# Moving the first block's bias lines behind the compression and the first FoX pair

## The chip, the cores and the metric

The kernel runs on one core of one Trainium2 chip. The time is device microseconds (us) of one execution. TensorE (PE, with its weight loads PEld) multiplies matrices, VectorE (DVE), ScalarE (ACT) and GpSimd (POOL) do the elementwise work, and SyncE (SP) issues most of the transfers (DMAs); POOL issues a few. Each engine works through its own instructions in order, and so does the queue from which it issues its DMAs: an instruction that waits for a semaphore holds up all that stand behind it on its engine.

## The reference, cut to what matters

Two transformer-like blocks, the first at sequence 512 and width 1024. The first mixes its tokens in three ways at once and then runs a convolutional feed-forward network; all is float32.

```python
h = rmsnorm(x, norm_g[0]) * (1 + sc_m) + sh_m
p_a, p_b, p_c = split_cols(h @ w_in, ...)
y_a = rwkv7_mix(p_a, ...)          # 4 heads, a recurrent scan over the tokens
y_b = fox_mix(p_b, b_f)            # 6 heads, softmax(q k^T + cum_q - cum_k), causal, 128-row blocks
y_c = nsa_mix(p_c, ..., rel_bias)  # 6 heads: compressed, selected and window attention
x = x + g_m * rmsnorm(concat(y_a, y_b, y_c) @ w_out, ...)
```

In `nsa_mix`, keys and values are first compressed (`gelu(flat @ w1) @ w2`, 31 compressed positions), and all logits get a bias that depends on the distance of two tokens alone: `rel_bias[t5_bucket(dist)]`, one value per head and distance. `mod`, from which `sc_m`, `g_m` and the like are cut, is `silu(c) @ ada_w`.

## The kernel before, in words

A float32 matrix product is made as three products of high and low parts (`uh`, `ul`, `whi`, `wlo`). A scheduler places the instructions: it takes the order in which the program names them as their priority, so that the program's order settles which of several ready instructions goes first on an engine, and the order of an engine's queue is fixed when the kernel is built.

The change lies in the RWKV stage of the first block, some 145 to 376 us into the span. The loop `while cores` (L1130) runs there in turns. A turn advances the two RWKV scans (`core(0)`, `core(1)`; their small matmuls go to PSUM tiles `psr`), adds matmuls of a projection as filler (`fill`, tiles `psm`, 128x512 outputs), every second turn one column group of `mod` (`some_ada`: 512 KB of weights into `raw`, products on DVE and on POOL, L507 and L508, adding up in `am`, and a matmul into `psr`), and takes NS = 3 steps of the list `side`. A step is what lies between two `yield`s of a generator. `side` holds, one behind the other:

- `compress`: for the keys and then the values, load `kcv` from SBUF into `kk2` (L970, L971), add position vectors on POOL (`kr`, L975), load four weight tiles `w1` (L980), and multiply (`psa<-kr,w1`).
- `fox(0)`, `fox(1)`, `fox(2)`: two heads each. For each of four blocks of 128 query rows and each head: logits into a PSUM tile of bank s (`pss<-fk,fq`, with 128, 256, 384 and 512 keys), minimum and bias on DVE (L1028), exponential on ACT, reciprocal on DVE, scaling on POOL (L1093), PE transposes into bank s (`pss<-cm,p`, L1052), a copy out (`pt`), and after both heads the product with the values (`psa<-pt,fv`). Bank s has two buffers.
- `stacks`: stacked copies of keys for NSA.

Ahead of the loop `decays(spare)` (L938) makes FoX's cumulated decays, `cum`, which go to DRAM (`dcum`, L958) and come back as bias tiles `fb` (L1081). Its last three statements are what the change moves:

- `lines("1", ...)` (L457): a table `lines1` of 33 rows, with one column per distance, comes in four chunks (512, 512, 512 and 96 columns: `lo<-in_lines`, L467), is cast on DVE (L469), multiplied on PE with the high and the low part of `rel_bias` (`pss<-lo,rb1h` and `rb1l`, 6 rows out, in bank s), copied by ACT (`lo<-pss`), and written to DRAM as `d1` (`d<-lo`, L475).
- `load_cb()` (L930): eight small DMAs on SP from `d1` to the tile `cb` (L935).
- `skew("k1", ...)` (L479): one DMA on POOL's queue that copies `d1` 128 times (1917 KB) into the DRAM tensor `k1`.

`cb` and `k1` are read in `nsa(j)`, behind the loop (L1174 and the `soften` of the compressed logits), from some 380 us on. The tiles named `lo`, `kk2`, `kr`, `w1`, `pt` come from `spare`, which hands out the RWKV stage's own tiles, five buffers in turn. `OR` is 0, so that `compress` stands first in `side`. The function `bias_1` is new with the change.

Of the kernel before, what the change touches and what calls it, by code (L numbers as in the profile page):

```python
# [279 lines left out]
def two_blocks(ctx, tc, ins, out):  # L280
    nc = tc.nc
    S, V, G, PE = nc.scalar, nc.vector, nc.gpsimd, nc.tensor
    def mm(o, l, r, start=True, stop=True):
        PE.matmul(o, l, r, start=start, stop=stop)  # L284

    def act(o, i, f, **kw):
        S.activation(o, i, f, **kw)  # L287

    def tt(o, a, b, op):
        V.tensor_tensor(o, a, b, op=op)  # L290

    def ts(o, a, s1, s2, op0, op1=ALU.bypass):
        if s2 is None:
            V.tensor_scalar(o, a, s1, None, op0=op0)
        else:
            V.tensor_scalar(o, a, s1, s2, op0=op0, op1=op1)

    def stt(o, a, s, b, op0, op1):
        V.scalar_tensor_tensor(o, a, s, b, op0=op0, op1=op1)  # L299
# [24 lines left out]
    def vc(name, i=0, n=1):  # L324
        s = VECS[name].start
        return vec[:, s + i:s + i + n]
# [129 lines left out]
    def lines(name, pool, o_tile, pst, rb, n, h, dst):  # L456

        l = pool.tile([33, h], F32, name="rb" + name)
        V.memset(l[32:33, :], 1.0)
        nc.sync.dma_start(l[:32, :], ins[rb])  # L460
        hi, lo = [pool.tile([33, h], F32R, name="rb" + name + c) for c in "hl"]
        act(hi, l, AF.Copy)
        tt(lo, l, hi.bitcast(F32), SUB)
        for j in range(0, n, 512):
            m = min(512, n - j)
            o = o_tile(F32)[:33, :m]
            nc.sync.dma_start(o, ins["lines" + name][:, j:j + m])  # L467
            E = o_tile(F32R)[:33, :m]
            (V if name == "1" else G).tensor_copy(E, o)  # L469
            ps = pst()[:h, :m]  # L470
            mm(ps, hi, E, True, False)
            mm(ps, lo, E, False, True)
            o = o_tile(F32)[:h, :m]
            act(o, ps, AF.Copy)
            nc.sync.dma_start(dst[:, j:j + m], o)  # L475

    def skew(name, src, row0, rows, rstep, off, n):

        d = dram.tile([rows, P, n], F32, name=name)  # L479
        s = src[:]  # L480
        w = s.shape[1]
        G.dma_start(d, bass.AP(tensor=s.tensor, offset=s.offset + row0 * w + off, ap=[[rstep * w, rows], [0, P], [1, n]]))
        return d
# [94 lines left out]
    def bank(tag, n):  # L578
        return psm.tile([P, T], F32, name="ps" + tag, tag="p" + tag, bufs=n)
# [328 lines left out]
    def project(jobs):  # L908
        for j in jobs:
            yield from j  # L910
# [22 lines left out]
    def load_cb():  # L933
        for p1 in range(8):
            nc.sync.dma_start(cb[p1 * 16:(p1 + 1) * 16],  # L935
                              bass.AP(tensor=d1[:].tensor, offset=d1[:].offset + LN + 7 - p1,
                                      ap=[[LC, 16], [E1_N, 6], [1, 55]]))

    def decays(spare):

        cf = spare("cf")[:, :P]
        nc.sync.dma_start(cf, ins["cmat"][:, CM["causT"]])
        V.tensor_copy(cmask[:, :P], cf)
        V.tensor_copy(cmask[:, P:], ident)
        ps = bank("s", 2)
        for b in range(NB):
            PE.transpose(ps[:6, b * P:(b + 1) * P], ffl[:, b], ident)
        f = spare("ff")
        act(f[:6], ps[:6], AF.Identity, bias=vc("b_f")[:6])
        na = spare("fa")  # L950
        act(na[:6], f[:6], AF.Abs)
        act(na[:6], na[:6], AF.Exp, scale=-1.0)
        act(na[:6], na[:6], AF.Ln, bias=1.0)
        stt(f[:6], f[:6], 0.0, na[:6], MIN, SUB)
        V.memset(na[:6], 1.0)
        cum = spare("cum")
        V.tensor_tensor_scan(cum[:6], na[:6], f[:6], 0.0, op0=MUL, op1=ADD)
        nc.sync.dma_start(dcum, cum[:6])  # L958
        lines("1", keep, lambda dt: spare("lo", dt), lambda: bank("s", 2), "rel_bias", E1_N, 6, d1)
        load_cb()  # L960
        k1.append(skew("k1", d1, 0, 6, 1, 0, LN))

    def compress(spare):

        for j, nm in enumerate(("k", "v")):
            pe = vc("pe_" + nm, 0, 16)
            krs = [spare("kr") for _ in range(2)]
            for g in range(2):
                kk = spare("kk2")
                nc.sync.dma_start(kk[0:64], kcv[j][H2[g]])  # L970
                nc.sync.dma_start(kk[64:128, :T - 1], kcv[j][H2[g], 1:])  # L971
                kv = kk.rearrange("p (c j l) -> p c j l", j=8, l=2)[:, :, :, 0].rearrange("p c j -> p j c")
                for a in range(2):
                    kr = krs[a][:, :496].rearrange("p (j g c) -> p j g c", g=2, c=31)
                    G.tensor_tensor(kr[:, :, g], kv[:, :, a:a + 31],  # L975
                                    pe[:, 8 * a:8 * a + 8, None].to_broadcast([P, 8, 31]), op=ADD)
            ps = bank("a", 1)
            for q in range(4):
                w1 = spare("w1")
                nc.sync.dma_start(w1, ins[f"c{nm}1"][:, q * T:(q + 1) * T])  # L980
                for a in range(4):
                    yield
                    mm(ps[:, :62], w1[:, a * P:(a + 1) * P], krs[q // 2][:, (4 * (q % 2) + a) * 62:(4 * (q % 2) + a + 1) * 62],
                       q + a == 0, q + a == 6)
            yield
            w2 = st.tile([P, 64], F32, name="w2")
            nc.sync.dma_start(w2, ins[f"nsa_c{nm}_w2"])
            h = st.tile([P, 62], F32, name="ch")
            V.tensor_copy(h, ps[:, :62])
            u = st.tile([P, 62], F32, name="cu")  # L990
            tt(u, h, h, MUL)
            ts(u, u, 0.044715, 1.0, MUL, ADD)
            tt(u, u, h, MUL)
            act(u, u, AF.Tanh, scale=math.sqrt(2.0 / math.pi))
            ts(u, u, 0.5, 0.5, MUL, ADD)
            tt(h, u, h, MUL)
            ps = bank("a", 1)
            if j == 0:
                for g in range(2):
                    mm(ps[H2[g], :31], w2, h[:, g * 31:g * 31 + 31])  # L1000
                V.tensor_copy(kct, ps[:, :31])
            else:
                for g in range(2):
                    mm(ps[:31, g * 64:g * 64 + 64], h[:, g * 31:g * 31 + 31], w2)
                V.tensor_copy(vcn.rearrange("c g d -> c (g d)"), ps[:31, :128])
        ts(gates[:, 0, 0:18:3], gates[:, 0, 0:18:3], valid, None, MUL)
# [55 lines left out]
    def stack_k(src, tiles, *room):  # L1062

        hl = parts(src, *room)
        r = []
        for s in range(2):
            k = tiles[2 * s:2 * s + 2]
            for a, b in zip(k, hl):
                nc.sync.dma_start(a[0:64].bitcast(F32), b[H2[s]].bitcast(F32))
                nc.sync.dma_start(a[64:128].bitcast(F32), b[H2[s]].bitcast(F32))  # L1070
            r.append(k)
        return r
# [30 lines left out]
    def stacks(spare):  # L1103
        for _ in work[0]:
            pass
        ka = [keep.tile([P, T], F32R, name="ksw", tag=t) for t in ("kcv0", "kcv1", "fk0", "fk1", "fk2")]
        kb = keep.tile([P, 3, T], F32R, name="ksw3", tag="fv")
        for src, tiles in ((ks, ka[:4]), (kw, [ka[4], *(kb[:, i] for i in range(3))])):
            kst.append(stack_k(src, tiles, *(spare("s" + c, F32R) for c in "hl")))
            yield  # L1110

    kst = []
    prep, core, spare = rwkv(phA.enter_context(tc.tile_pool(name="rp", bufs=1, reuse_waits="tile")))
# [7 lines left out]
    nm[0] = 1  # L1121
    work[0] = project(jobs[NA:])
    decays(spare)
    side = [*(fox(j, spare) for j in range(3))]
    side.insert(OR, compress(spare))
    side.append(stacks(spare))
    side = project(side)
    turn = [0]
# [876 lines left out]
```

## Time and profile before

| | |
|---|---|
| median of 3 runs | 2211.7 us (2207.88 to 2213.74) |
| profiled execution | 2211.9 us, span 2210.1 us |
| PE busy | 2137.1 us, 97% of the span |
| DVE, ACT, POOL busy | 1167.0, 799.1, 465.2 us |
| mean granted TensorE clock | 0.977 |

PE busy counts a matmul that runs at the lower of the clock's two levels (1.2 and 2.4 GHz, shown as 0.5 and 1.0) as busy for its longer time. In the rows below, the same matmul therefore appears with two durations, and a stretch's column PEclk is the mean of the level granted in it. Names are shown without their buffer numbers: `w` is `w1`, `cb<-d` reads `d1`, `k<-d` is `k1<-d1`, `raw<-in_ada_dram` a group of `mod`'s weights. `psa<-kr,w` counts each matmul in two parts.

### The profile page before, as it was taken

Reading aid. Unit: us, or ns where it says so; the run is one execution under the profiler, and the core shown is the slowest. Engines: PE = TensorE matmul, PEld = TensorE weight load, DVE = VectorE, ACT = ScalarE, POOL = GpSimd, SP = SyncE. Lnnn points to the kernel's source line nnn. Section 1 sums busy time; section 2 is a strip of 40 time slices with the busy share of each in tenths; the row PEclk is TensorE's granted clock in tenths of the full one; section 3 lists DMA queues with packets and bytes.
Section 4 is the critical chain, followed back from the end, with each engine's and each line's share of the span. In section 5 each row is a group of like instructions: output and inputs, shape, how many; then the busy total and the mean of one; then the engine's idle time right before and its main releaser. Section 6 shows DMA issues by size and latency. Waiting matters only on the chain.

```text
span 2210.1 us, 31599 instructions
## 1 busy us (share of the span) xinstructions
PE 2137.1 (97%) x12444; PEld 1764.5 (80%) x12444; DVE 1167.0 (53%) x2217; ACT 799.1 (36%) x1358; POOL 465.2 (21%) x459
## 2 busy tenths in 40 slices
PE   5988999997999999899999999999999999999999
PEld 4867776766788888888888889998877888888887
DVE  8563544567653464654344439967655455433442
ACT  5432323452543343432222325445453233222221
POOL 5044342325000000321011023343221022100110
PEclk9988998997999999999999999999999999999999
DMA  7245334200452222132222343243162223222222
GB/s 271 91 139 184 106 125 123 88 1 32 151 182 96 95 96 98 55 113 97 95 95 96 120 142 112 93 138 95 67 186 70 101 84 101 102 96 96 95 96 86
DMA packets 84975, 238.32 MB, mean 108 GB/s; under 512 B 14032, under 2 KB 21510, under 8 KB 84698
## 3 DMA queue, kind: packets, MB, share of 16 engines
q1 hardware_dynamic: 79098, 226.41, 30.5%
q0 software_dynamic: 5008, 9.31, 1.2%
q8 instruction: 98, 1.61, 0.3%
q10 hardware_dynamic: 720, 0.57, 0.1%
q14 instruction: 51, 0.42, 0.1%
HBM read 216.02 MB, written 15.33 MB: 105 GB/s over the span
## 4 chain that ended last, share of the span: by engine, by line
PE 91%; DVE 4%; DMA 3%; ACT 1%; issue 1%; POOL 1%; SPq 0%; DVEq 0%; ACTq 0%; POOLq 0%
PE mm L284 67%; PE psm L284 6%; PE psr L284 4%; PE pS L284 3%; PE pss L284 2%; PE pso L284 2%; PE pO L284 2%; PE k L284 1%; PE psa L284 1%; PE pT L1590 1%; PE pst L1052 1%; DMA aw<-in_ada_dram 1%; DMA raw<-in_wst_dram 1%; PE pT L1573 1%; DVE ul L299 1%
## 5 line engine op out<-in xcount | busy, mean ns | idle before, releaser
L273 ACT ACTIVATE whi<-raw 128x1024 fp32r<-128x1024 f32 (+4 forms) x314 | 327.6, 1046 | 815.7 <-PE mm L284 622.9
L274 DVE TENSOR_TENSOR wlo<-raw,whi 128x1024 fp32r<-128x1024 f32 (+4 forms) x302 | 370.7, 1229 | 337.8 <-ACT whi L273 325.0
L284 PE MATMUL mm<-ul,whi 128*128 128x512 f32 (+1 forms) x1296 | 501.9, 388 | 5.5 <-DVE ul L299 5.5
L284 PE MATMUL mm<-uh,wlo 128*128 128x512 f32 (+1 forms) x1296 | 501.5, 388 | 1.0 <-DVE wlo L274 1.0
L284 PE MATMUL mm<-uh,whi 128*128 128x512 f32 (+1 forms) x1296 | 496.6, 388 | 4.3 <-ACT uh L287 3.3
L284 PEld LDWEIGHTS mm<-ul,whi 128*128 128x128 f32 x1296 | 244.9, 189 | 58.5 <-DVE ul L299 8.2
L284 PEld LDWEIGHTS mm<-uh,whi 128*128 128x128 f32 x1296 | 243.3, 189 | 56.0 <-ACT uh L287 4.7
L284 PEld LDWEIGHTS mm<-uh,wlo 128*128 128x128 f32 x1296 | 244.9, 189 | 50.9 <-DVE wlo L274 1.9
L284 PE MATMUL mm<-hh,wlo 128*128 128x512 f32 (+1 forms) x550 | 209.3, 381 | 0.0
L284 PE MATMUL mm<-hl,whi 128*128 128x512 f32 (+1 forms) x550 | 209.3, 381 | 0.0
L284 PE MATMUL mm<-hh,whi 128*128 128x512 f32 (+1 forms) x550 | 208.4, 381 | 0.0
L1441 POOL TENSOR_TENSOR gg<-gg,R 128x512 f32<-128x512 f32 x44 | 77.5, 1763 | 473.4 <-ACT gg L287 473.4
L284 PE MATMUL mm<-whi,uh 128*128 128x256 f32 (+1 forms) x488 | 140.5, 288 | 0.0
L284 PE MATMUL mm<-whi,ul 128*128 128x256 f32 (+1 forms) x488 | 139.8, 287 | 0.0
L284 PE MATMUL mm<-wlo,uh 128*128 128x256 f32 (+1 forms) x488 | 139.2, 285 | 0.0
L284 PEld LDWEIGHTS mm<-hl,whi 128*128 128x128 f32 x550 | 103.4, 188 | 19.8
L284 PEld LDWEIGHTS mm<-hh,wlo 128*128 128x128 f32 x550 | 103.4, 188 | 19.7
L284 PEld LDWEIGHTS mm<-hh,whi 128*128 128x128 f32 x550 | 103.4, 188 | 19.7
L287 ACT ACTIVATE p<-p,smin 128x128 f32<-128x128 f32 (+4 forms) x136 | 81.8, 602 | 82.3 <-DVE smin L1028 45.8
L290 DVE TENSOR_TENSOR gh<-mm,gg 128x512 f32<-128x512 f32 x44 | 30.4, 691 | 130.5 <-PE mm L284 124.9
L284 PEld LDWEIGHTS mm<-whi,ul 128*128 128x128 f32 x488 | 93.1, 191 | 1.7 <-issue 1.5
L284 PEld LDWEIGHTS mm<-whi,uh 128*128 128x128 f32 x488 | 93.0, 191 | 1.4 <-issue 0.4
(509 smaller groups left out, 3419.3 us busy)
## 6 DMA issues: line engine op xcount, KB each, us to landing
raw<-in_wst_dram SPq DMA_DIRECT2D x294, 512.0 KB
raw<-in_ada_dram SPq DMA_DIRECT2D x32, 512.0 KB
aw<-in_ada_dram SPq DMA_DIRECT2D x16, 512.0 KB
raw<-in_wst_dram SPq DMA_DIRECT2D x8, 448.0 KB
ka<-d POOLq DMA_DIRECT2D x1, 3570.0 KB, 51.5
k<-d POOLq DMA_DIRECT2D x1, 2556.0 KB, 20.6
part<-in_x_dram SPq DMA_DIRECT2D x4, 512.0 KB
xa<-in_x_dram SPq DMA_DIRECT2D x8, 256.0 KB
```

The lines of the kernel that those rows point to most:

```text
L273: nc.scalar.activation(hi[:, :n], w, AF.Copy)
L274: (e or nc.vector).tensor_tensor(lo[:, :n], w, hi[:, :n].bitcast(F32), op=ALU.subtract)
L284: PE.matmul(o, l, r, start=start, stop=stop)
L287: S.activation(o, i, f, **kw)
L290: V.tensor_tensor(o, a, b, op=op)
L299: V.scalar_tensor_tensor(o, a, s, b, op0=op0, op1=op1)
L1052: PE.transpose(ps[:, j:j + P], p[:, j:j + P], ident)
L1441: G.tensor_tensor(g, g, R, op=MUL)
L1573: PE.transpose(ps[:, (j * nb + b) * P:(j * nb + b + 1) * P], xn[:, (b * n + j) * P:(b * n + j + 1) * P], ident)
L1590: PE.transpose(ps[:, j:j + P], p[:, o + j:o + j + P], ident)
```

## The change

Three statements of `decays` become a generator `bias_1`, which goes into `side` at position 2: behind `compress` (0) and `fox(0)` (1), ahead of `fox(1)`. It has two steps: the lines, and then `load_cb` with `skew`.

```diff
         V.tensor_tensor_scan(cum[:6], na[:6], f[:6], 0.0, op0=MUL, op1=ADD)
         nc.sync.dma_start(dcum, cum[:6])
+
+    def bias_1(spare):
+
         lines("1", keep, lambda dt: spare("lo", dt), lambda: bank("s", 2), "rel_bias", E1_N, 6, d1)
+        yield
         load_cb()
         k1.append(skew("k1", d1, 0, 6, 1, 0, LN))
+        yield
 
     def compress(spare):
...
     side = [*(fox(j, spare) for j in range(3))]
     side.insert(OR, compress(spare))
+    side.insert(2, bias_1(spare))
     side.append(stacks(spare))
```

The number of instructions stays the same; their order changes. Line numbers behind `decays` grow by five (L975 is what L970 was), and buffer numbers by a constant in each part. The first place is SP's queue at the head of the stage, with the last writes of `d1`, the eight `cb` loads and the compression's loads. Before:

```order
L475 DMA d1_93<-lo_1216 6x512
L497 DMA raw_2048<-in_ada_dram 128x1024
L497 DMA raw_2054<-in_ada_dram 128x1024
L970 DMA kk2_1276<-kcv0_109 64x512
L475 DMA d1_93<-lo_1226 6x96
L971 DMA kk2_1276<-kcv0_109 64x511
L497 DMA raw_2280<-in_ada_dram 128x1024
L935 DMA cb_654<-d1_93 16x6x55 x8
L970 DMA kk2_1281<-kcv0_109 64x512
L971 DMA kk2_1281<-kcv0_109 64x511
L980 DMA w1_1287<-in_ck1_dram 128x512
L980 DMA w1_1342<-in_ck1_dram 128x512
```

And now, nearer to the queue's start:

```order
L975 DMA kk2_1219<-kcv0_109 64x512
L976 DMA kk2_1219<-kcv0_109 64x511
L497 DMA raw_1675<-in_ada_dram 128x1024
L958 DMA dcum_653<-cum_1179 6x512
L975 DMA kk2_1224<-kcv0_109 64x512
L976 DMA kk2_1224<-kcv0_109 64x511
L985 DMA w1_1230<-in_ck1_dram 128x512
L985 DMA w1_1285<-in_ck1_dram 128x512
```

The first weight tiles of the compression have gone 18 rows up in the queue, ahead of everything that `lines` and `load_cb` issue, and stand behind `dcum` and the loads of `kk2`.

The second place is PE, where the first matmuls of the compression stand among those of the RWKV scans. Before:

```order
L284 MATMUL psr1_1776<-X_1498,part_89 64x64 x11
L284 MATMUL psa_1286<-kr_1274,w1_1287 128x62 x4
L284 MATMUL psa_1286<-kr_1274,w1_1342 128x62 x4
L284 MATMUL psr1_1776<-X_1498,part_89 64x64 x3
```

And now:

```order
L284 MATMUL psr0_1322<-part_89,pr0_113 64x128 x8
L284 MATMUL psr1_1332<-part_89,pr1_114 64x128 x4
L284 MATMUL psa_1229<-kr_1217,w1_1230 128x62 x4
L284 MATMUL psa_1229<-kr_1217,w1_1285 128x62 x4
L284 MATMUL psr1_1332<-part_89,pr1_114 64x128 x4
```

The `psa` rows have gone 62 rows up PE's order, to the scans' 64x128 matmuls.

The third place is POOL's queue between `fox(0)` and `fox(1)`; `p_2602` and `p_2617` are `fox(1)`'s first two scalings. Now:

```order
L507 TENSOR_SCALAR raw_3286<-raw_3286,sil_79 128x256 x3
L508 TENSOR_TENSOR am1_3042<-am1_3042,raw_3049 128x256 x3
L512 TENSOR_TENSOR am1_3042<-am0_3041,am1_3042 128x256
L482 DMA k1_2548<-d1_93 768x1x639
L508 TENSOR_TENSOR am1_3279<-am1_3279,raw_3286 128x256 x3
L512 TENSOR_TENSOR am1_3279<-am0_3278,am1_3279 128x256
L507 TENSOR_SCALAR raw_3489<-raw_3489,sil_79 128x256 x3
L1098 TENSOR_SCALAR p_2602<-p_2602,srec_2607 128x128
L508 TENSOR_TENSOR am1_3482<-am1_3482,raw_3489 128x256 x2
L1098 TENSOR_SCALAR p_2617<-p_2617,srec_2622 128x128
```

Before, the `k1` DMA stood 41 rows further up, at the head of the stage, among the additions for `am1_1731`. On PE the four pairs of `pss<-lo` now stand between `fox(0)`'s last `psa<-pt,fv` and `fox(1)`'s first logits, which stood ahead of that `psa` before. Behind the last filler matmul of the loop, PE now has `fox(1)`'s last logits, its last two groups of transposes and all eight logits and transposes of `fox(2)`; before it had `fox(2)`'s last four logits and five groups of transposes.

## Rows read from the trace of the kernel before

**Rows 1.** The page, parts 1 and 4: busy time, chain of waits.

```profile
PE 2137.1 (97%) x12444; PEld 1764.5 (80%) x12444; DVE 1167.0 (53%) x2217; ACT 799.1 (36%) x1358; POOL 465.2 (21%) x459
...
PE 91%; DVE 4%; DMA 3%; ACT 1%; issue 1%; POOL 1%; SPq 0%; DVEq 0%; ACTq 0%; POOLq 0%
```

**Rows 2.** Windows: length, then busy of five engines, PEclk, DMA share, GB/s.

```profile
180.00:220.00 40.00, 32.87 (x381) 28.99 (x381) 11.13 (x28) 8.22 (x13) 17.34 (x28) 0.74 0.61 186
...
300.00:340.00 40.00, 38.12 (x397) 28.57 (x392) 19.66 (x56) 10.23 (x22) 16.21 (x26) 0.96 0.45 155
340.00:380.00 40.00, 38.37 (x274) 24.61 (x274) 17.87 (x44) 13.57 (x27) 11.23 (x11) 0.79 0.32 91
```

**Rows 3.** Waits of PE, 140 to 400 us: total, times, longest.

```profile
PE psa L284 <- DMA w<-in_ck_dram: 7.1, 1, 7.1
...
PE pss L1052 <- POOL p L1093: 1.9, 2, 1.7
```

**Rows 4.** The chain that ended last, 160 to 200 us: start, duration, piece.

```profile
173.92 7.72 DMA d<-lo
...
181.69 5.33 DMA cb<-d
...
188.23 3.28 DMA w<-in_ck_dram
```

**Rows 5.** Timeline of PE, 150 to 216 us: start, duration, instruction, idle before.

```profile
157.86 1.96 PE L284 MATMUL psr<-part,pr 64*64 64x128 f32 x32
```

**Rows 6.** Timeline of PE behind the wait for `w`.

```profile
191.65 3.64 PE L284 MATMUL psa<-kr,w 128*128 128x62 f32 x16 [7.13 <-DMA w<-in_ck_dram]
...
196.43 0.63 PE L284 MATMUL psm<-ul,whi 128*128 128x512 f32 x1
...
209.62 0.39 PE L284 MATMUL psm<-ul,whi 128*128 128x512 f32 x1
```

**Rows 7.** Timeline of SP's queue, 145 to 200 us.

```profile
151.29 0.29 SPq L958 DMA_DIRECT2D dcum<-cum  x1
```

**Rows 8.** Timeline of POOL, 145 to 200 us.

```profile
183.00 1.42 POOL L975 TENSOR_TENSOR kr<-kk,vec 128x248 f32<-128x248 f32 x2 [1.26 <-DMA kk<-kcv]
```

**Rows 9.** Groups by line and form, 145 to 200 us: busy, mean ns, idle before.

```profile
L284 PE MATMUL pss<-lo,rb1l 33*6 33x512 f32 x3 | 1.4, 470 | 0.0
```

**Rows 10.** DMA issues, 140 to 200 us: count, KB each, us to landing.

```profile
k<-d POOLq DMA_DIRECT2D x1, 1917.0 KB, 21.6
```

**Rows 11.** Timeline of DVE, 170 to 190 us.

```profile
176.51 0.35 DVE L294 TENSOR_SCALAR am<-raw,sil 128x256 f32<-128x256 f32 x1 [4.26 <-DMA raw<-in_ada_dram]
...
185.98 0.74 DVE L294 TENSOR_SCALAR am<-raw,sil 128x256 f32<-128x256 f32 x1 [7.56 <-POOL am L512]
```

**Rows 12.** Timeline of PE at 308.7 us and behind it.

```profile
308.71 0.55 PE L1052 MATMUL pss<-cm,p 128*128 128x128 f32 x3 [1.69 <-POOL p L1093]
```

**Rows 13.** Timeline of PE and POOL, two FoX steps with 384 and 512 keys.

```profile
249.76 0.91 PE L284 MATMUL pss<-fk,fq 64*128 64x384 f32 x2
252.52 0.59 POOL L1093 TENSOR_SCALAR p<-p,srec 128x384 f32<-128x384 f32 x1 [0.18 <-DVE srec L1036]
254.22 1.12 PE L284 MATMUL pss<-fk,fq 64*128 64x512 f32 x2
257.51 0.70 POOL L1093 TENSOR_SCALAR p<-p,srec 128x512 f32<-128x512 f32 x1 [4.40 <-PE psr L284]
```

**Rows 14.** Timeline of PE, the stage's end: last filler, last FoX step, next stage.

```profile
344.78 0.39 PE L284 MATMUL psm<-uh,wlo 128*128 128x512 f32 x1
...
365.37 2.07 PE L284 MATMUL pss<-fk,fq 64*128 64x512 f32 x2
...
371.95 1.09 PE L1052 MATMUL pss<-cm,p 128*128 128x128 f32 x4
373.84 1.97 PE L284 MATMUL psa<-pt,fv 128*64 128x128 f32 x14 [0.80 <-DVE pt L1046]
...
376.31 0.79 PE L284 MATMUL psm<-uh,whi 128*128 128x512 f32 x1
```

## The prediction

> **What bounds the kernel now.** I read the page first: PE is busy for 97% of the span and holds 91% of the chain of waits [rows 1], so a change of order can move the time only where PE stands idle or runs at the lower level of its clock. The table by stretches shows where that is in the RWKV stage. From 180 to 220 us PE is idle for 7.1 of 40 us, and the granted clock has a mean of 0.74; from 300 to 340 us 1.9 us are idle at a mean of 0.96; from 340 to 380 us 1.6 us at 0.79 [rows 2]. The list of PE's waits names the causes: one wait of 7.1 us of the compression's matmuls for the DMA of `w`, and two for POOL's scaling of `p`, 1.9 us together [rows 3]. The chain of waits follows the long one back: the last write of `d1` takes 7.72 us to land, SP stands on the `cb` loads that wait for it until 181.69, these and the `kk` loads behind them go out up to 188.23, and `w` then takes 3.28 us [rows 4]. The reader should see that PE waits for a transfer that is short but was issued late, behind one that nobody needs for another 190 us.
>
> PE then goes on at the lower level: a filler matmul takes 0.63 us at 196.43 and 0.39 at 209.62 [rows 6]. A mean of 0.74 over 40 us, with levels 1.0 and 0.5, is 20.8 us at the lower one; 7.1 of these were the wait itself, so 13.7 us of work ran at half speed and lost 6.9 us.
>
> **The change, part by part.** The sum is made against the profiled execution: 2211.9 us, of which 2210.1 are span; the median of 2211.7 is 0.2 below it.
>
> *What it removes.* Neither `d1`'s writes nor the `cb` loads stand ahead of the compression's loads now. `dcum`, which stands just ahead of them, was issued at 151.29 [rows 7]; two `kr` additions take 1.42 us [rows 8], and `w` lands 3.28 us after its issue [rows 4]. With the loads of `kk` issued some us earlier and landed by then, I estimate `w` at 151.3 + 0.3 + 1.4 + 3.3, about 156.5 us. PE comes to the moved `psa` in the middle of the row that began at 157.86 [rows 5], which itself comes earlier by the first pair of `lines` matmuls, about 1 us. So the wait ends between 0 and 1 us long. Term: -7.1 for the wait and -6.9 for the clock, -14.0 together. Its bounds are 0, if a wait of the same kind comes back further on, and -14.0.
>
> *What comes back at once.* The compression's second half (the values) needs the same tiles of `spare` again; its loads of `kk` wait for `kr` tiles, which are free only when PE has used up the first half. Their trip (`kk`, `kr`, `w`) has no slack in the new order, where PE wants the result after about 20 us. Bounds: 0, and the 7.1 us that the same kind of wait cost before [rows 3]. I take +3, somewhat nearer to 0, since no long transfer of `d1` stands in that trip.
>
> *The lines themselves.* The eight matmuls of some 0.47 us [rows 9], the casts and the copies are the same ones in another place. On PE they cost the same; a chunk's trip is hidden by the filler between two pairs of `pss<-lo`. 0, with 0.5 either way, the wait for `lo` that exists now being of that size.
>
> *POOL and the DMA queues between* `fox(0)` *and* `fox(1)`. The `k1` DMA now stands in POOL's queue in front of `fox(1)`'s first scaling, and waits there for writes of `d1` to land, one of which took 7.72 us [rows 4]. Behind it on POOL are three additions for `am1_3279`, the scaling of `raw_3489` (which waits for its own load) and then `p_2602`, for which PE's first transposes of `fox(1)` wait; behind these the next loads of `raw` on SP, since they want the tiles back. No row of before shows POOL held up right ahead of a FoX step for long. The nearest is the wait of 1.69 us at 308.71 [rows 12]; with it goes a mean clock of 0.96 over 40 us, 1.6 us more [rows 2], so 3.3 in all. The farthest is DVE's wait of 7.56 us for POOL while `k1` was under way [rows 11]. Two first scalings are at risk: bounds 0 and 2 x (7.6 + 1.6) = 18.4. I take two times the nearest row, +6.6.
>
> A second reason lies in the transfers. `k1` took 21.6 us to land [rows 10], and while it was under way DVE waited 4.26 us for a load of `raw` [rows 11]; until now this ran beside a stage with slack on DVE, and now it runs beside FoX. The Trainium skill, page "DMA: Bandwidth & Descriptors", section "Issuing engines are not separate DMA queues", says that DMAs of all issuing engines run on the same 16 DMA engines and interleave, so that POOL's queue gives `k1` no road of its own. By that rule the slow `raw` loads move with `k1` to the new place, and the term stands; if `k1` had a road of its own, the later of the two waits and its 3.3 us would go. The wait of 4.26 us agrees with the rule, without proving it.
>
> *The end of the stage.* `side` is a chain: two more steps behind `fox(0)` put `fox(1)` and `fox(2)` later against the filler matmuls, which are used up earlier. Behind the last filler there now stand nine FoX steps instead of the five of before, and nothing but the scans' own work beside them. A step with 384 keys takes 3.35 us from its logits at 249.76 to the end of its scaling [rows 13], and three transposes take 0.55 [rows 12]: 3.9 us. One with 512 keys takes 3.99 from 254.22 [rows 13], and four transposes by the same measure some 0.7: 4.65. By that slope of 0.75 I estimate 3.15 and 2.4 us for 256 and 128 keys. Nine steps are 4.65 + 2 x (2.4 + 3.15 + 3.9 + 4.65) = 32.9, and the last `psa` 1.97: 34.8 us, against 31.5 us from 344.78 to 376.31 before [rows 14], so +3.3. But the PE work of four more steps, which I estimate at 6 us (logits of 0.5 to 1.1, transposes and `psa` of about as much), leaves the stretch ahead of the last filler: -2.7. The other bound: at the lower clock the last step took from 365.37 to 373.04, 7.7 us instead of 4.65 [rows 14], 1.65 times as much; if the four last steps (17.1 us) ran so without cover, 11.1 us more, or +8.4. I take +3.
>
> *Sum.* -14.0 + 3 + 6.6 + 3 = -1.4: 2210.5, rounded to **2210 us** on the scale of the median.
>
> **The rivals.** A measurement of this kernel can tell about 0.3% from no change, 6.6 us.
>
> *Given back only at the tail (faster).* POOL's queue is held up no longer than PE has other work: the scans' matmuls between `fox(1)`'s first logits and its transposes cover it, as they cover all FoX steps but two now [rows 3]. Then -14.0 + 0 to 3 for the values' half, 0 at POOL, and -2.7 to +3 at the tail. The middle is about -12: 2200 us, from 2195 to 2205. For it: DVE and POOL are far from full. Against it: POOL works in order, and `k1` waits for `d1` now in front of a scaling.
>
> *POOL held up behind* `k1` *(slower).* If the write of `d1` for which `k1` waits lands as late as before (7.72 us) and each of `fox(1)`'s two first scalings comes late by the farthest row, the zone costs +18.4 and with the rest 2222 us; with the tail's upper bound, 2228. This decides as soon as the two waits are together more than about 15 us. For it: the long wait of DVE for POOL in just such a constellation. Against it: that row is DVE's wait, not PE's, and no row shows two such waits one after the other.
>
> *The change doesn't do what it says.* The late `w` stays, since the values' half waits instead: 7.1 us and the clock come back, the removal is worth 0, and the zone and the tail stand alone: 2211.9 + 6.6 + 3, 2221 us. For it: the same five tiles are handed round in `spare`. Against it: no `d1` write stands in front of those loads any more.
>
> **How the numbers follow.** My forecast, the return of most of the gain, has a chance of 0.46, with a range of its own from 2203 to 2218; the faster rival 0.31, `k1` 0.14, the wait that stays 0.09. Of the forecast's chance 0.03 lie on the faster side and 0.03 on the slower. The faster rival's 0.31 count as 0.29 faster and 0.02 the same; the two slower ones' 0.23 as 0.20 slower and 0.03 the same. Faster 0.32, within 0.3% 0.45, slower 0.23. The range takes in the forecast and the nearer part of the rivals, 2199 to 2222.
>
> **What would show it.** In the profile of the changed kernel the wait of `psa<-kr,w` for `w` should be gone, and the filler matmuls behind it should take 0.39 us from the start; that is the part I am surest of. SP should issue `w` by about 154 us. POOL should show a gap ahead of `k1` and the list of PE's waits a longer `pss<-cm,p` for `p` at `fox(1)`'s start, 3 to 4 us twice with the clock. From the last filler to the next stage's first should be 33 to 40 us. The forecast is wrong if `fox(1)`'s first transposes wait for less than 1 us (then faster), or if `psa` waits for `w` again in the values' half by more than 5 us (then slower).

## The result: slower by 1.0%, and the profile after

| | before | changed |
|---|---|---|
| median, us | 2209.82 (4 runs, same chip) | 2234.98 (4 runs) |
| ratio, 95% interval | | 1.0101 [1.0086, 1.0115] |
| span of the profiled execution, us | 2210.1 | 2233.7 |
| mean granted TensorE clock | 0.977 | 0.969 |

The prediction was 2210 us within 2199 to 2222. The measured time lies outside, on the slower side. The ratios, here and below, are those on record for the fast executions and not quotients of the medians (1.0114 here); one execution of e4_kct_act (2661.89 us) and one of e13_last_chunk_end (11735.5 us) are left out of them.

All of the difference arises in the RWKV stage. Here is the table by stretches of both kernels, cut where each begins the next stage's matmuls (columns as in [rows 2]); first the kernel before:

```profile
145.00:376.30 231.30, 216.08 (x2541) 163.47 (x2539) 110.54 (x280) 69.54 (x141) 96.11 (x140) 0.90 0.42 138
...
620.00:2210.10 1590.10, 1577.53 (x8116) 1333.97 (x8114) 801.87 (x1359) 554.72 (x837) 256.14 (x191) 1.00 0.31 103
```

The changed kernel, the stage as a whole, and then what follows some 244 us behind its end, as above:

```profile
145.00:401.20 256.20, 225.08 (x2536) 169.40 (x2536) 110.28 (x280) 69.33 (x140) 95.21 (x139) 0.83 0.38 123
...
645.00:2233.70 1588.70, 1575.28 (x8113) 1332.48 (x8111) 800.30 (x1359) 554.43 (x836) 255.37 (x191) 1.00 0.31 103
```

The stage is 24.9 us longer, with the same instructions. PE is idle for 31.1 us in it, where it was 15.2: 15.9 us. It is busy for 225.1 us, where it was 216.1, since the mean clock fell from 0.90 to 0.83: 9.0 us. From there to the end of the span it is 1832.5 us, where it was 1833.8.

The same view of the changed kernel, cut at the places where something happens:

```profile
145.00:187.80 42.80, 31.02 (x444) 26.29 (x444) 27.49 (x53) 10.96 (x17) 28.94 (x36) 0.86 0.63 197
...
271.40:312.00 40.60, 29.54 (x347) 22.50 (x347) 10.94 (x30) 10.24 (x23) 15.50 (x24) 0.80 0.45 149
...
349.80:401.20 51.40, 45.31 (x325) 27.04 (x323) 19.87 (x59) 16.10 (x36) 13.06 (x17) 0.67 0.21 62
```

The last of these stretches, in the kernel before:

```profile
344.78:376.30 31.52, 29.89 (x242) 18.09 (x240) 15.06 (x38) 10.54 (x21) 9.10 (x9) 0.77 0.27 78
```

Three stretches stand out: the compression's end (187.8), the stretch between `fox(0)` and `fox(1)`, with 11.1 us of idle PE, and the end of the stage, 51.5 us from the last filler to the next stage instead of 31.5 [rows 14], at a mean clock of 0.67 instead of 0.77. PE's waits by what ended them, 140 to 430 us, answer to [rows 3]:

```profile
PE pss L1057 <- POOL p L1098: 10.1, 5, 2.8
PE psa L284 <- DVE kct L1006: 7.4, 1, 7.4
PE psr L284 <- DVE MT L290: 6.3, 1, 6.3
...
PE psa L284 <- DVE pt L1051: 2.8, 2, 2.0
PE psa L284 <- DMA w<-in_ck_dram: 1.2, 1, 1.2
```

The wait for the keys' `w`, 7.1 us in [rows 3], is down to 1.2. In its place stands one of 7.4 us for `kct`, and those for `p`, `MT` and `pt` did not exist in this size.

**The compression.** From the timelines of SP, POOL, DVE and PE of the changed kernel, in that order:

```profile
169.97 6.72 SPq L497 DMA_DIRECT2D raw<-in_ada_dram  x3
176.86 0.47 SPq L975 DMA_DIRECT2D kk<-kcv  x1
...
181.69 1.39 POOL L980 TENSOR_TENSOR kr<-kk,vec 128x248 f32<-128x248 f32 x2 [3.66 <-DMA kk<-kcv]
183.04 2.32 POOL L508 TENSOR_TENSOR am<-am,raw 128x256 f32<-128x256 f32 x3
...
186.20 0.35 DVE L294 TENSOR_SCALAR am<-raw,sil 128x256 f32<-128x256 f32 x1 [7.77 <-POOL am L512]
187.50 0.18 DVE L1006 COPY kct<-psa 128x31 f32<-128x31 f32 x1
...
187.79 1.51 PE L284 MATMUL psa<-kr,w 128*128 128x62 f32 x6 [7.44 <-DVE kct L1006]
```

Read it from the bottom. PE waits for the copy of `kct`, which frees the one buffer of bank a. The copy takes 0.18 us, but stands on DVE behind a product for `am`, which waits for POOL, which waits for the values' `kk`, which SP issued at 176.86 behind three loads of `raw`. It is a wait of the same length as the one removed, 4 us earlier in the span. The granted clock falls during the wait in both kernels. In the windows of the kernel before (first the wait's beginning, then the work behind it):

```profile
184.50:187.70 3.20, 0.02 (x1) 0.00 (x0) 1.65 (x4) 0.00 (x0) 2.00 (x3) 1.00 0.32 81
...
191.70:208.20 16.50, 16.50 (x140) 14.76 (x142) 5.07 (x11) 2.82 (x3) 6.05 (x11) 0.50 0.70 224
```

And in the changed kernel, behind its wait:

```profile
187.80:200.00 12.20, 12.20 (x95) 10.40 (x97) 2.54 (x6) 3.13 (x5) 4.44 (x7) 0.50 0.58 189
```

It is at the lower level once more from 224.0 to 230.7 us, with 6.2 us of work. Half of such work is lost time: some 8 us before, some 9 now.

**Between fox(0) and fox(1).** From the timelines of POOL, DVE and PE:

```profile
282.75 1.33 POOL L482 DMA_DIRECT2D k<-d  x1 [6.56 <-DMA d<-lo]
299.11 1.39 POOL L507 TENSOR_SCALAR raw<-raw,sil 128x256 f32<-128x256 f32 x3 [11.37 <-DMA raw<-in_ada_dram]
...
295.09 0.35 DVE L294 TENSOR_SCALAR am<-raw,sil 128x256 f32<-128x256 f32 x1 [9.72 <-DMA raw<-in_ada_dram]
...
287.77 0.45 PE L284 MATMUL pss<-fk,fq 64*128 64x128 f32 x2
297.66 0.47 PE L284 MATMUL psr<-WU,pr 64*64 64x64 f32 x2 [6.28 <-DVE MT L290]
300.90 0.47 PE L1057 MATMUL pss<-cm,p 128*128 128x128 f32 x1 [2.76 <-POOL p L1098]
```

DVE stands for 9.72 us on a load of `raw`, with `MT` of the scans behind it, for which PE waits. POOL stands for 11.37 us on the next load, with `fox(1)`'s `p` behind it. And `fox(1)`'s first logits come at 287.77 us, 68.6 us behind `fox(0)`'s first:

```profile
219.15 0.48 PE L284 MATMUL pss<-fk,fq 64*128 64x128 f32 x2
```

Before, the two were 43.2 us apart:

```profile
224.94 0.49 PE L284 MATMUL pss<-fk,fq 64*128 64x128 f32 x2
...
268.18 0.49 PE L284 MATMUL pss<-fk,fq 64*128 64x128 f32 x2
```

From 272 to 291 us, where the four links run, PE has no wait at all: it works off the scans and filler.

**The end.** PE's timeline, last filler, last FoX steps, next stage:

```profile
349.75 0.40 PE L284 MATMUL psm<-uh,wlo 128*128 128x512 f32 x1
...
384.80 0.90 PE L1057 MATMUL pss<-cm,p 128*128 128x128 f32 x3 [1.79 <-POOL p L1098]
...
396.87 1.11 PE L1057 MATMUL pss<-cm,p 128*128 128x128 f32 x4 [2.19 <-POOL p L1098]
...
401.23 0.80 PE L284 MATMUL psm<-uh,whi 128*128 128x512 f32 x1
```

Nine FoX steps run behind the last filler; their logits stand at 350.68, 356.56, 359.64, 362.74, 366.51, 373.13, 380.52, 385.63 and 391.77 us. Three of the last four steps wait for their own chain (logits, minimum, exponential, scaling), and PE is idle for 6.1 us of the stretch, where it was 1.6. From 367.4 us to its end, 33.8 us, the granted clock is at its lower level, where it was so for 14.4 us before (from 361.9): four transposes take 1.11 us, like the 1.09 in [rows 14].

### The profile page after: what moved, and what is told of

It reads as the page before. It is cut to its first block, busy times and chain, and to the rows that moved or that the text cites. A ratio compares the mean times of both kernels' runs of the same rounds, so it can differ in the third digit from the quotient of the medians.

```text
span 2233.7 us, 31606 instructions
## 1 busy us (share of the span) xinstructions
PE 2144.7 (96%) x12444; PEld 1768.9 (79%) x12444; DVE 1165.5 (52%) x2217; ACT 800.6 (36%) x1358; POOL 464.6 (21%) x459
## 4 chain that ended last, share of the span: by engine, by line
PE 89%; DVE 5%; DMA 3%; POOL 1%; ACT 1%; issue 1%; SPq 0%; DVEq 0%; POOLq 0%; ACTq 0%
PE mm L284 66%; PE psm L284 5%; PE psr L284 3%; PE pS L284 3%; PE pss L284 2%; PE pso L284 2%; PE pO L284 2%; DMA raw<-in_ada_dram 1%; PE k L284 1%; PE pT L1596 1%; PE pst L1057 1%; PE psa L284 1%; DMA aw<-in_ada_dram 1%; DVE am L299 1%; DVE ul L299 1%
```

## The experiments

All stand against the kernel before on the same chip, whose median in these sessions was 2212.3 to 2212.8 us, some 3 us above the one in the result; a time that misses an expected range by less than that says little. In the table, *gap* is the time from `fox(0)`'s first logits to `fox(1)`'s, *end* that from the last filler to the next stage, *compression* the sum of PE's waits ahead of `psa<-kr,w`, all from the profiled execution, in us.

| kernel | links between fox(0) and fox(1) | k1 issued at | gap | end | compression | ratio [95%] |
|---|---|---|---|---|---|---|
| before | 0 | 165.2 | 43.2 | 31.5 | 7.1 | 1 |
| changed | 4 | 282.8 | 68.6 | 51.5 | 8.6 | 1.0101 [1.0086, 1.0115] |
| e4_kct_act | 4 | as changed | 68.0 | 51.5 | 8.1 | 1.0100 [1.0082, 1.0117] |
| e6_double | 4 | 163.8 | 67.1 | 50.0 | 8.6 | 1.0073 [1.0050, 1.0096] |
| e19_bank_a | 4, in bank a | 282.2 | 45.2 | 42.8 | 7.2 | 1.0023 [1.0013, 1.0034] |
| e7_one_link | 1 | 274.8 | 53.1 | 38.9 | 3.1 | 1.0012 [1.0003, 1.0021] |
| e16_in_fox1 | 0 (1 in fox(1)) | 309.2 | 47.7 | 35.3 | 4.3 | 1.0023 [1.0012, 1.0034] |
| e17_in_fox2_early | 0 (1 in fox(2)) | 338.3 | 47.3 | 37.0 | 2.6 | 0.9993 [0.9984, 1.0002] |
| e15_in_fox2 | 0 (1 in fox(2)) | 345.5 | 46.3 | 34.4 | 3.9 | 0.9982 [0.9972, 0.9993] |
| e13_last_chunk_end | 0 | 163.4 | 43.8 | 31.8 | 6.6 | 0.9984 [0.9973, 0.9995] |
| e10_mid | 0 | 207.5 | 63.7 | 33.0 | 8.9 | 1.0041 [1.0027, 1.0055] |
| e5_last | 0 | 381.2 | 46.7 | 40.1 | 9.5 | 1.0088 [1.0072, 1.0105] |

A link is one chunk of `lines`: load, cast, two matmuls, copy, write.

**e4_kct_act: is it the copy's place in DVE's queue?** The changed kernel with

```diff
-                V.tensor_copy(kct, ps[:, :31])
+                act(kct, ps[:, :31], AF.Copy)
```

> The changed kernel with one edit: the compressed keys (kct) are copied out of PSUM by ACT instead of DVE. In the changed kernel the values' half of the compression waits 7.4 us for that copy, which stands on DVE behind an addition for am that waits for POOL. Theory A (the copy's place in DVE's queue makes the wait): the wait falls below 2 us, and with the clock the time falls by 7 to 13 us, to 2222 to 2228. Rival (the operands kr and w of the values' half come late anyway): the wait stays at 5 us or more under another name, and the time stays within 3 us of 2235.

2235.83 us, ratio 1.0100, the same as the changed kernel. The rival holds. The wait of PE has another name and the same length:

```profile
186.60 1.51 PE L284 MATMUL psa<-kr,w 128*128 128x62 f32 x6 [7.11 <-DMA w<-in_cv_dram]
```

The profile puts a wait down to what came last. Here two things came almost together, and taking one away moved nothing: the values' `kk`, `kr` and `w` follow one another, and the whole trip was late.

**e6_double: the links without k1.**

```diff
+        lines("1", ..., d1)
+        k1.append(skew("k1", d1, 0, 6, 1, 0, LN))
+
     def bias_1(spare):
 
-        lines("1", ..., d1)
+        lines("1", ..., d1b)
         yield
         load_cb()
-        k1.append(skew("k1", d1, 0, 6, 1, 0, LN))
```

> The lines are made twice: at the head of the stage, where k1 is copied from them as in the kernel before, and again behind fox(0), where cb alone reads them. So the four links of lines stand in FoX's chain as in the changed kernel, but the 1917 KB of k1 do not move there. Theory A (two separate prices behind fox(0): k1's transfer slows the loads of raw, and the links use up time that FoX then lacks at the stage's end): loads of raw between fox(0) and fox(1) land in 3 to 5 us instead of 7 to 8, PE's waits there fall from 11 us to under 4, but the stretch from the last filler to the next stage stays above 43 us; time 2212 to 2224. Rival B (k1's transfer makes all of the loss, and the long end is only its consequence): the end goes back to 31 to 36 us and the time to 2200 to 2210.

2225.9 us, ratio 1.0073, 2 us above the upper end of theory A's range and far from rival B. The gap stays at 67.1 us and the end at 50.0, without any of `k1`'s bytes moving there. So the links alone hold FoX back, and the long end is theirs. PE's waits between 260 and 312 us fall from 11.1 to 5.4, not under 4 as expected; 2.9 of the 5.4 are for the link's `lo`. The loads of `raw` come sooner: DVE's longest wait for one there is

```profile
288.27 0.35 DVE L294 TENSOR_SCALAR am<-raw,sil 128x256 f32<-128x256 f32 x1 [4.70 <-DMA raw<-in_ada_dram]
```

instead of 9.72. The waits show a part of `k1`'s transfer in the loss. The times don't show it clear of noise: the two ratios differ by 0.28%, but their intervals overlap. This kernel also makes the lines twice, which may hide some of that part.

**e7_one_link: one link, with k1.** Only the second chunk of `lines`, with what needs it, stays in `bias_1`:

```diff
+        lines("1", ..., d1, (0, 2, 3))
+
     def bias_1(spare):
 
-        lines("1", ..., d1)
+        lines("1", ..., d1, (1,))
```

> Three of the four chunks of lines stay at the head of the stage; only the second chunk, with load_cb and the k1 copy (which both need it), goes behind fox(0). So one link instead of four stands in FoX's chain, with k1's transfer beside it as in the changed kernel. Theory A: the waits for raw and for am stay (PE waits 6 to 11 us between fox(0) and fox(1)), but the end of the stage shortens from 51 to 36 to 42 us; time 2216 to 2226. Rival B (k1 makes all of the loss): both stay, the time is 2230 or more. Rival C (links make all of the loss): the waits shrink with them, 2205 to 2212.

2214.24 us, ratio 1.0012, between the ranges of A and C. The end is 38.9 us, inside theory A's 36 to 42. The time is 2 us below its range (the compression waits for 3.1 us only, 4 less than before, so that the 0.12% is what is left after that gain). PE's waits from 260 to 312 us are 3.9 us, not 6 to 11, though `k1` moves there as in the changed kernel. The loads are slow here too: POOL waits 8.27 us for `raw` (until 295.19), DVE 5.24. But `fox(1)`'s first three scalings stand ahead of that wait on POOL, at 273.80, 280.08 and 286.45 us, while in the changed kernel the first stands behind it, at 300.48. So A was wrong on the size of `k1`'s part: its slow loads cost PE much where the links have put `fox(1)`'s scalings behind them. Four links against one: gap 68.6 against 53.1, end 51.5 against 38.9.

**e19_bank_a: by what do the links hold FoX?** One word of the changed kernel:

```diff
-        lines("1", ..., lambda: bank("s", 2), "rel_bias", E1_N, 6, d1)
+        lines("1", ..., lambda: bank("a", 1), "rel_bias", E1_N, 6, d1)
```

> The changed kernel, but the four matmul results of lines go to PSUM bank a (one buffer, which FoX uses only for its products with the values) and not to bank s. Theory A1 (FoX waits for the links because both take turns in bank s): fox(1)'s first logits come about 43 to 46 us behind fox(0)'s first, as before the change, not 69; the end of the stage falls to 36 to 42 us; time 2215 to 2224. Theory A2 (the links hold FoX by the five tiles of spare as well, from which both lo and pt are handed out): the first logits come early as above, but those with 256 keys come no earlier than in the changed kernel, the end of the stage stays at 45 us or more, and the time at 2226 to 2236.

2217.61 us, ratio 1.0023: this word gives back about three quarters of the loss. The first logits of `fox(1)` come 45.2 us behind `fox(0)`'s, so bank s was what held them. One word of the source changes the order on the other engines too: `fox(1)`'s first two scalings now stand on POOL at 271.87 and 274.97 us, ahead of `k1` (282.18) and of the 10.83 us that POOL waits for `raw` behind it. So the three quarters take in a part of what `k1` cost. The end is 42.8 us, between the ranges of A1 and A2, and the logits with 256 keys come late still:

```profile
265.81 0.49 PE L284 MATMUL pss<-fk,fq 64*128 64x128 f32 x2
...
296.02 0.94 PE L284 MATMUL pss<-fk,fq 64*128 64x256 f32 x2
```

30.2 us apart, where before they are at 268.18 and 280.42, 12.2 us apart. The trace shows where: the two transposes ahead of them are done by 278.5 us, but their copies out (`pt`) come at 292.22 on ACT, right behind the last link's copy (292.07), and at 295.22 on DVE, behind a wait for `raw` that ends at 294.43. What puts them there was not tried; the five shared tiles of `spare` (both `lo` and `pt` come from them) and bank a's one buffer, which `psa<-pt,fv` needs, are both left.

**e13_last_chunk_end: the stall alone.** As before the change, but the fourth chunk and `load_cb` go behind `fox(2)`:

```diff
-        lines("1", ..., d1)
-        load_cb()
+        lines("1", ..., d1, (0, 1, 2))
         k1.append(skew("k1", d1, 0, 6, 1, 0, LN))
+
+    def bias_1(spare):
+        lines("1", ..., d1, (3,))
+        yield
+        load_cb()
+        yield
...
+    side.append(bias_1(spare))
     side.append(stacks(spare))
```

> As before the change, but the fourth chunk of lines (96 columns) and load_cb, which needs it, go behind fox(2); the other chunks and k1 stay at the head. This takes away the one thing for which SP stood still ahead of the compression's loads, and puts next to nothing into FoX's chain. Theory A (the gain is real, the price lies in what stands between fox(0) and fox(1)): the 7.1 us wait for w falls below 2 us, the end of the stage stays at 30 to 34 us, and the time is 2197 to 2204. Rival (the compression's values then wait, as they do for 7.4 us in the changed kernel, so that the gain does not exist): 2207 to 2213.

2208.16 us, ratio 0.9984: a gain of 0.16%, at the lower end of the rival's range. The wait for `w` did not go, 6.6 us are left. SP issued the two `w` in time, from 171.32 us on, but the chain of waits shows why that was of little use:

```profile
172.01 13.06 DMA w<-in_ck_dram
```

256 KB took 13.06 us to land, where the kernel before needed 3.28 [rows 4]. Not all of that is `k1`'s: two loads of `raw` (512 KB each) went out here from 166.85 us on, just ahead of the `w`, while the last one before it had gone 10 us earlier in the kernel before. `k1` was issued at 163.4 and took 21.5 us. In the kernel before, `k1` left at 165.2 and had landed after 21.6 us, just ahead of `w`'s issue at 188.23: the stalled `cb` loads had kept `w` out of its way.

**e15_in_fox2: neither cb nor k1 beside the compression.** As e7_one_link, with `bias_1` inside `fox(2)`:

```diff
+    def mixed(g, at):
+        for n, _ in enumerate(g):
+            yield
+            if n == at:
+                yield from bias_1(spare)
...
+    side[2] = mixed(side[2], 5)
     side.insert(OR, compress(spare))
-    side.insert(2, bias_1(spare))
```

> Three of the four chunks of lines stay at the head of the stage; the second chunk, load_cb and the k1 copy go into the middle of fox(2), behind its steps with 256 keys. So neither the cb loads nor k1's 21 us of transfer run beside the compression's loads, only one link stands in FoX's chain, and it stands where the queues are nearly empty. Theory A (k1 in flight makes the compression's w late, and what stands between fox(0) and fox(1) makes the rest of the loss): the wait for w falls below 2 us, the values' half waits at most 4 us, the end of the stage stays at 30 to 35 us; time 2194 to 2203. Rival (the compression waits for kk, kr and w of its own, wherever k1 is; the gain does not exist): PE still waits 6 us or more there, 2207 to 2214. Second rival (k1 comes too late for the bias tiles tb of NSA): the compression's wait is gone, but NSA's first steps wait 5 us or more, 2203 to 2212.

2208.66 us, ratio 0.9982. `k1` is issued at 345.5. The wait for `w` is spread over three short ones, 2.5 us together, and the compression costs 3.9 us in all. The chain of waits has a `w` that went out beside loads of `raw`, without `k1`:

```profile
175.03 7.27 DMA w<-in_ck_dram
```

So some 6 of the 13.06 us in e13_last_chunk_end can be put down to `k1`, an estimate from these two rows. The second rival fails: PE's longest wait in NSA's first 100 us is 0.8 us. The time is above theory A's 2194 to 2203 all the same. Part of the saving is paid back at the end:

```profile
367.46 1.12 PE L1060 MATMUL pss<-cm,p 128*128 128x128 f32 x4 [4.65 <-POOL p L1101]
```

There the last logits were done by 359.8 us, but their minimum on DVE came at 364.75, behind the additions for the scans' output `y`: the order there has changed too, and the end is 34.4 us instead of 31.5. `k1` is not what PE waits for.

**e17_in_fox2_early and e16_in_fox1: the same, earlier.** `mixed(side[2], 2)` and `mixed(side[1], 8)` in the edit above.

> As the run with one link in fox(2), but three steps earlier, behind the steps with 128 keys. There PE waited 4.65 us for POOL's scaling at 367 us, near the end. Theory A: k1 moves some 10 us earlier, that wait falls below 3 us, while one more group of FoX stands behind the last filler (end of the stage 34 to 38 us); time 2204 to 2210, no different from there by more than 0.2%. Rival (k1 in flight made the late wait and the rest is free): 2199 to 2203.

2210.08 us, ratio 0.9993, no difference from before that can be told. The late wait is 2.1 us, but the end is 37.0 us: one thing is traded for the other, as theory A said.

> As the run with one link in fox(2), but the second chunk, load_cb and k1 stand in fox(1), behind its steps with 384 keys. Theory A (a link costs what it delays FoX before the filler is used up, and k1 costs what its transfer delays): the compression's wait is as small as there (under 4 us together), k1 slows the loads of raw in fox(1), so that PE waits 3 to 8 us there, and the end of the stage is 34 to 38 us; time 2206 to 2213. Rival (in fox(2) k1's time beside the end of the stage was the larger price): 2198 to 2205.

2217.2 us, ratio 1.0023, slower than both and above the expected range. The end is 35.3 us as expected, the compression's wait 4.3 instead of under 4; in `fox(1)` PE waits 2.0 us for the link's `lo`, ahead of `k1`, and 1.8 us for the scans' `NF` beside it, so less than the 3 to 8 us expected of `k1`. What makes the rest of the 0.4% against e15_in_fox2 is open.

**e10_mid: all of it inside the compression.** `bias_1` whole, run at `compress`'s 21st step.

> All of bias_1 as in the changed kernel, but run inside compress, early in its values' half, and not behind fox(0). FoX's chain is as before the change, and k1 moves beside the values' loads and fox(0)'s start. Theory A: nothing of the changed kernel's loss between fox(0) and fox(1) and at the end of the stage (30 to 35 us) is left, but the values' half waits as long as in the changed kernel or longer (7 to 12 us), since its w loads stand behind writes of d1 and beside k1; time 2205 to 2215. Rival (the place behind fox(0) costs nothing by itself, the lines do wherever they stand): 2225 or more.

2220.65 us, ratio 1.0041, 6 us above the range. The end is 33.0 us, and nothing is lost between the FoX pairs, as expected. In the keys' half PE waits 7.9 us for `ch` (the second product's input, not counted in the table): DVE stands for 10.12 us on the load of the lines' first chunk, with `cu` and `ch` behind it. The values' half waits 6.8 us for its `w`, which stand on SP behind `d1`'s writes (one of 6.73 us to landing) and the `cb` loads (6.71). The lines there cost in the compression, though less than behind `fox(0)` (0.41% against 1.01%). The gap of 63.7 us in the table is no link's: `fox(0)`'s first logits run ahead of the values' half there.

**e5_last: behind all of FoX.** `side.append(bias_1(spare))` in place of the `insert`. It stands behind `fox(2)` and ahead of the stacks; the expectation has that last point wrong.

> bias_1 unchanged, but as the last but nothing of the list: behind fox(2) and the stacks. FoX's chain is as before; the links run one after the other behind fox(2)'s logits, and k1 moves only when NSA begins. Theory A: PE waits for kr, w or kct in the values' half about 7 us as in the changed kernel, nothing between fox(0) and fox(1), and the end of the stage is 31 to 40 us; then NSA's first steps wait for k1's 21 us, of which the projection's filler covers a part; time 2212 to 2230. Rival (all of the loss is the lines' work in any new place): 2235.

2230.93 us, ratio 1.0088, just above theory A's range. FoX is as before (gap 46.7), but the loss appears at a new place: 4.2 us of waits for `lo` at the end of the stage, which is 40.1 us long, and 7.3 us in NSA for `qs`, whose loads (issued at 408.07) stand behind `cb`'s and those of the stacks on SP.

## Why the prediction was wrong, step by step

- **The removal (-14.0) came, and came back whole.** The wait for the keys' `w` fell to 1.2 us, next to the 0 to 1 worked out. But the step "what comes back at once (+3)" was mis-sized: the values' half waits 7.4 us, just above the upper bound, and the clock is low behind it as it was before, for which the step had no term. (The clock's own term was read a little low: 7.1 of the 20.8 us at the lower level were taken for the wait, but the clock was still high up to 187.7, and 16.5 us of work ran low, some 8 us lost and not 6.9.) `fox(0)` ended 1 us earlier than before, not 11. That was the forecast's fourth case, "the wait that stays", with a chance of 0.09, and its sign on record, more than 5 us in the values' half, came. e4_kct_act shows that the copy's place on DVE does not make that wait, and e13_last_chunk_end that even the keys' `w`, issued in time, lands late beside `k1` and loads of `raw`. A wait that is taken away gives nothing when the same trip is made a second time right behind it, as late as before.
- **POOL and the queues (+6.6): right in place, but the smaller part of a larger price.** PE's waits there were 11.1 us. The mechanism is the one named, loads of `raw` slowed by `k1` and an in-order engine behind them, though DVE was hit before POOL. Without `k1` there (e6_double) 5.4 us of the waits are left, and a ratio of 1.0073. From `fox(0)`'s last logits (260.93 before, 260.13 now) to the last filler the stage became 5.8 us longer, with five FoX steps fewer in it.
- **The end of the stage (+3): this is the step that failed.** It came out 20.0 us longer, against bounds of -2.7 to +8.4. Two errors. The first is a comparison of unlike things: nine steps were summed at the price that a step has at full clock with other work beside it (34.8 us), and set against the stretch as measured before (31.5 us). The count was unlike too: nine is that of the logits, five that of the groups of transposes. There are nine logits and ten groups now, four and five before, so five more steps and not four. At the same prices the four logits of before come to 2 x 3.9 + 2 x 4.65 + 1.97 = 19.1 us, so that 12 us of the old stretch were already outside these prices; like with like, five more steps are +15.7, not +3.3. As measured, the nine took 50.6 us from the first logits to the next stage (the three from 366.51 on, for instance, 6.6, 7.4 and 5.1 us instead of 3.15, 3.9 and 3.9). The second: the relief of "6 us of PE work" ahead of it was counted as gained time, though PE then stood idle between the FoX pairs instead. The nine logits behind the last filler were right.
- **The cause was named too weakly: "two more steps".** It is not the steps but the links. Each needs a load, a cast, matmuls, a copy, and takes turns with FoX's logits in bank s; four of them put `fox(1)` back by 25 us (gap 68.6 against 43.2), one by 10 (e7_one_link). The prediction held the lines' own cost for 0, "hidden by the filler". They were: the filler hid them and was then missing at the end. e19_bank_a, whose source differs in the bank alone, takes away three quarters of the loss, `k1`'s share among it, and is the shortest proof that bank s holds FoX there.
- **The rivals.** That of `k1` at POOL had its place right and its price wrong: e7_one_link has `k1` there, and 0.12% of loss, with a compression that waits 4 us less. None of the four cases had the end of the stage as its main term.

How the loss splits among the three by size is shown only roughly: the links carry most (e6_double keeps them and 0.73% of loss), `k1` beside them perhaps a quarter (the 0.28% of e6_double, with overlapping intervals), and the compression gives nothing back. The first two are not separate prices either: with one link, or with bank a, `fox(1)`'s first scalings go ahead of `k1`'s slow loads, and most of both is gone.

## What to carry to other kernels

Work that is cheap on every engine is still dear if it takes a buffer in a chain whose end is covered by filler: ask which ring of buffers the moved work joins, and how many of its round trips then stand ahead of the chain. A wait for a DMA that was issued late may have been keeping that DMA out of the way of another; look what is in flight at the time to which it would move. And count filler as something that is used up: what covers a stall here is missing there.

## What the runs showed of the hardware that was not expected

A 256 KB load took 13.06 us to land with the 1917 KB of `k1` in flight (e13_last_chunk_end), against 3.28 us without it [rows 4] and 7.27 us without it but beside loads of `raw` (e15_in_fox2), though `k1` was issued from POOL's queue and the load from SP's. That one queue's transfer slows the other's agrees with what the Trainium skill, page "DMA: Bandwidth & Descriptors", section "Issuing engines are not separate DMA queues", says: they run on the same 16 DMA engines. By how much, the prediction had taken from waits of 4 to 8 us; beside the same transfer POOL stood 8.27 us on a load of `raw` in e7_one_link too, and PE waited 3.9 us in all from 260 to 312 us.
